# Regrouping the small products of a recurrence by shape and by array half

## The chip, the cores and the metric

The kernel runs on one core of one Trainium2 chip. The metric is the device time of the program in microseconds (us), the median of several runs. The profile comes from one further execution of the same program, taken by the hardware profiler.

## The reference

Two layers of a block on 256 tokens of width 2048, in fp32: a mixer with two branches (an RWKV-7 recurrence with 16 heads of 64, and a causal attention with 8 heads), a cross attention on 256 memory rows, and a feed-forward part of width 8192. The change lies in the recurrence, which the reference writes token by token:

```python
def step(state, inp):
    r_t, w_t, k_t, v_t, kk_t, b_t = inp
    sa = jnp.einsum('bhvk,bhk->bhv', state, -kk_t)
    state = (state * w_t[:, :, None, :]
             + sa[..., :, None] * b_t[:, :, None, :]
             + v_t[..., :, None] * k_t[:, :, None, :])
    return state, jnp.einsum('bhvk,bhk->bhv', state, r_t)
```

Each head then has a group norm over its 64 outputs, a bonus term and a gate. The result is joined with the attention's output and goes through the output projection.

## The kernel before

**Main line and fibers.** Instructions of TensorE are issued in the order in which the program emits them. The large products are the main line (`gemmA`, `gemmB`, `gemm_seq`): weights of 512 columns are loaded as fp32 (`raw`), split by ScalarE into a rounded high part `wh` (line 298) and by VectorE into the rest `wl` (lines 300 and 304), and multiplied in three terms, which accumulate in PSUM tiles named `g`. Everything else on TensorE runs in fibers: Python generators that yield an estimate in microseconds, or an event, until their next TensorE instruction can run. `K.clk` is a planned clock: `mm` (line 237) adds an estimated cost for each product, and after each k tile of a large product (128 rows of the weights) `poll` steps the fibers whose time has come. The planner thus weaves small products between large ones. Fibers put their products in PSUM tiles named `x`, from a pool of four banks (`xps`); `half` is half of such a bank. All products go through `mm`, so their line in the profile is L243; transpositions are L248. The other engines take their instructions in their own order.

**The recurrence in chunks.** A layer's 16 heads are worked in two groups of eight (`g`), the 256 tokens in four chunks (`c`) of 64. Of a group's eight heads four (`h` = 0) lie on partitions 0 to 63 of the operands and four (`h` = 1) on partitions 64 to 127; `i` counts the four, `j` = 4h + i. The fibers of one group, in order:

- `f_group` (line 606) makes the decayed operands `AR` and `BK`, then runs `f_inner` (line 690). For each chunk `f_inner` multiplies `BK` by `AR` head by head (64 rows by 128 columns), first the four heads of one row half (`q` = 0), masked by VectorE into `W` (line 706), then a yield (line 708), then the other four. ScalarE copies parts of `W` to `G` (line 710). After the four chunks come the bonus, the transposed operands `tok` and the inverse, whose forward substitution `f_fs` (line 776) is on VectorE.
- `f_v` (line 800) prepares the values; in layer 1 it mixes in the first layer's values (lines 826 to 830, GpSimd, then VectorE) and transposes them.
- `f_chain` (line 859) takes the state from chunk to chunk in three products of eight heads each: `X` (line 873, from `W` and `V`), `SA` (line 882, from `UT` and `X`) and, but for the last chunk, the new state `Sn` (line 892, from `tok` and `V`). List `HD` (line 857) is the order of the heads: the four of the first half, then the four of the second. The halves of `X` and of `Sn` go to different column halves of the array (partitions 0 to 63 and 64 to 127 of one PSUM tile), those of `SA` come from different row halves. After chunks 1 and 3 it spawns `f_out`.
- `f_out` (line 908) is called for 128 tokens (`t`), two chunks. For each head half and chunk it computes, head by head, `W` times `VS` (128 rows by 64 columns of the array) and, in all chunks but the first, `AR` times the state (64 by 64), added to the same output (lines 926 and 928). VectorE takes mean and difference from the output (lines 929 to 931), a yield follows for each half, then group norm, transposition of `oc`, gate (`gup`, `gl`) and split.

The output projection `w_out` (line 1261) waits for `f_out` and the attention heads, k tile by k tile.

Of the kernel before, what the change touches and what calls it, by code (L numbers as in the profile page):

```python
# [12 lines left out]
ALU = mybir.AluOpType  # L13
AX = mybir.AxisListType

D, S, L = 2048, 256, 2
# [102 lines left out]
def pull(gen, n):  # L119
    """the first n of gen, now"""  # L120
    return [next(gen) for _ in range(n)]


def ahead(gen, n):
    """gen, made n items before their use"""
    buf = []
    for x in gen:
        buf.append(x)
        if len(buf) > n:
            yield buf.pop(0)  # L130
    yield from buf


class K:
    """PE instructions are issued in the order in which they are emitted here. The large products are the
    main line; everything else on PE runs in fibers, generators that yield an estimate of the time (us) until
    their next PE instruction can run, or the event they wait for."""
# [112 lines left out]
    def rsqrt(self, dst, src, scale, eps):  # L250
        """dst = (src*scale + eps)^-0.5, small tiles"""
        g = self.nc.gpsimd
        t = self.sm("rs", list(src.shape))
        g.tensor_scalar(out=t, in0=src, scalar1=scale, scalar2=eps, op0=ALU.mult, op1=ALU.add)
        g.tensor_tensor(out=dst, in0=t, in1=self.mhalf[:, : src.shape[-1]], op=ALU.pow)

# [1 line left out]
    def units(self, src, k0, nk, ncols, extra=None, heap=None, first=False):  # L258
        """yield (wh, wl, k tiles) of src[(k p), cols]"""
        nc = self.nc  # L260
# [19 lines left out]
    def hunits(self, w, nk, h0, nh, dh, hw, off):  # L280
        """units of head-strided columns: w[(k p), (h hw)] -> cols h*hw+off : +dh for nh heads"""
        nc = self.nc
# [32 lines left out]
    def gemm_seq(self, parts, lhs, order, need=None):  # L315
        """out[tok, N] = x @ w, parts: (units, number of k tiles, N, evac(t, ps)); order: (token tile, part, units) or
        (None, call, None);
        lhs(k, tok) -> (xh, xl) [128, 128]; need(k, tok): event before"""
# [25 lines left out]
    def gemmA(self, parts, nk, lhs, N, evac, need=None):  # L344
        """out[tok, N] = x @ w, both token tiles at a time; parts: generators of units"""
# [14 lines left out]
    def gemmB(self, units, nk, rhs, evac, nft=4, need=None):  # L360
        """out[feat, tok]: evac(pair, ps[128, 2, 256])"""
# [20 lines left out]
    def sumsq(self, srcs, name="ss"):  # L382
        """srcs: list of [128, n] APs -> [128, 1] sum of squares"""
# [16 lines left out]
    def toT(self, src, gain, U, t, j, nk=4):  # L400
        """src [128 tok, nk*128] -> k tiles 4j.. of U at the tokens of t, split; gain [128, k tiles]"""
# [23 lines left out]
    def load_bc(self, vec):  # L425
        """[2048] -> four [128, 512] tiles, the same on every partition"""
# [7 lines left out]
    def tiles4(self, s="y"):  # L434
        """[tok tile][512 columns]"""
# [10 lines left out]
    def f_pre(self, tag, l, h, t, gain, U, rstd, y=None, part=None):  # L446
        """h[t] += rms_norm(y[t]), then U (raw h * gain, transposed) and rstd[t] of h"""
# [13 lines left out]
    def finish(self, y, part, h, t):  # L461
        """h[t] += rms_norm"""
# [9 lines left out]
    def shift2(self, ps, scale_bc, mus, dests):  # L472
        """token shift of ps [P, n, 256] feature-major; dests: n [R, 256] APs"""
# [17 lines left out]
    def f_small(self, l, z, rstd, sm):  # L491
        """after the decay, learning rate, gate and value-residual columns z"""
        nc = self.nc
        yield ("z", l)
        # rstd[tok], the same on every partition
# [62 lines left out]
    def shift_gemm(self, l, g, c0, mu, U, sm, dst, key):  # L558
        """dst[128, 4, 256] = token shifted columns c0 + 512 g .. of the in projection, feature major"""
# [13 lines left out]
    def f_lora(self, l, g, sm, R):  # L573
        """lw = log decay, token major; a, feature major"""
# [8 lines left out]
        # -exp(-.5) * sigmoid(w0 + tanh(wl) @ w_up)  # L583
# [7 lines left out]
        # sigmoid(a0 + al @ a_up)  # L591
# [14 lines left out]
    def f_group(self, l, g, sm, R):  # L606
        """eight heads (columns 512 g ..): decayed operands, bonus, inverse"""
# [9 lines left out]
        # 1 / |kk| per head and token  # L617
# [25 lines left out]
        for i in range(4):  # L643
# [12 lines left out]
            # cumulative decays  # L656
# [33 lines left out]
    def f_inner(self, l, g, R, prods):  # L690
        """per chunk the masked products W [(b, k; s), head, (a, r; t)], the token-major b~, k~,
        and (I - Aab)^-1, transposed, in UT [(heads 0-3, 4-7; s), chunk, head, t]"""
# [5 lines left out]
        for c in range(4):  # L698
            W = self.t4("W", [128, 8, 128])
            for q in range(2):  # L700
                ps = self.xps().rearrange("p (h t) -> p h t", h=4)
                rows = slice(64 * q, 64 * q + 64)
                for i in range(4):
                    self.mm(ps[:, i, :], BK[i // 2][rows, i % 2, c].rearrange("p a b -> p (a b)"),
                            AR[i // 2][rows, i % 2, c].rearrange("p a b -> p (a b)"), True, True)
                nc.vector.tensor_tensor(out=W[:, 4 * q : 4 * q + 4, :], in0=ps, in1=mw, op=ALU.mult)
                if q == 0:
                    yield (0.60, 1.1)[g]
# [14 lines left out]
        # bonus, over the heads' keys  # L723
# [41 lines left out]
        # a~ in the place of Aab, above Aak  # L765
# [10 lines left out]
    def f_fs(self, l, g, N, T, R):  # L776
        """the inverses of the unit lower triangular 32 x 32 blocks, by forward substitution:
        T[(parity of the column, half, unit), row, column // 2]"""
# [13 lines left out]
        # Ud[(half, s), unit, t] = T[t, s], Tr[(half, t), unit, s] = T[t, s]  # L792
# [7 lines left out]
    def f_v(self, l, g, sm, R):  # L800
        """values: residual, token-major copies VS, bonus * v + lnx_b"""
# [55 lines left out]
    HD = [(h, i, 4 * h + i, slice(64 * h, 64 * h + 64)) for h in range(2) for i in range(4)]  # L857

    def f_chain(self, l, g, sm, R, O):
        """the state from chunk to chunk"""  # L860
# [6 lines left out]
        for c in range(4):  # L867
            W, V, St = Ws[c], VS[c], Sts[c]
            # X = A~ S' + Aak V, S' over V's rows 0-63
# [7 lines left out]
            # SA = T X, over V's rows 0-63  # L877
            for h in range(2):
                psa = self.half()
                rows = slice(64 * h, 64 * h + 64)  # L880
                for i in range(4):
                    self.mm(psa[0:64, i, :], UT[rows, c, i, :], X[rows, i, :], True, True)
                if h:
                    nc.vector.tensor_copy(out=V[0:64, 4:8, :], in_=psa[0:64])
                else:
                    nc.scalar.copy(out=V[0:64, 0:4, :], in_=psa[0:64])
            yield (1.8, 1.8)[g]
            if c < 3:
                # S' <- gamma (S' + B~^T SA + K~^T V)
# [18 lines left out]
    def f_out(self, l, g, t, sm, R, Sts, oh, ol):  # L908
        """O = R~ S' + Arb SA + Ark V, token major, group norm over the head dim, bonus, gate"""
# [8 lines left out]
        oc = self.t2("oc", [128, 4, 2, 64])  # L918
        for h in range(2):
            po = self.half()  # L920
            rows = slice(64 * h, 64 * h + 64)
            for c in (2 * t, 2 * t + 1):
                orow = slice(64 * (c % 2), 64 * (c % 2) + 64)
                for i in range(4):
                    j = 4 * h + i
                    self.mm(po[orow, i, :], Ws[c][:, j, 64:128], VS[c][:, j, :], True, c == 0, True)
                    if c:
                        self.mm(po[orow, i, :], AR[i // 2][rows, i % 2, c, 1, :], Sts[c][rows, i, :], False, True, True)
# [3 lines left out]
            yield (0.5, 0.5)[g]  # L932
# [25 lines left out]
    def mix(self, l, U, rstd, units):  # L958
        """the mixed tokens, transposed and split: a function of the k tile and the token tile"""
# [47 lines left out]
    def rope(self, x, t, dst, n, e):  # L1007
        """x, dst [128, n, 64]"""
# [511 lines left out]
```

## Time and profile before

| | |
|---|---|
| time, median of 3 runs | 2681.59 us (2678.27 to 2687.71) |
| the profiled execution, span | 2672.5 us |
| the two stretches with the recurrence's products | 130 to 452 us (layer 0), 1452 to 1781 us (layer 1) |
| ScalarE, VectorE, GpSimd busy | 45%, 60%, 16% |
| moved by DMA | 456.69 MB, mean 171 GB/s |

The profiled execution has no time of its own beside its span; the median of the runs stands 9.1 us above it. In the views `PE` is TensorE's matmuls, `PEld` its weight loads, `DVE` VectorE, `ACT` ScalarE, `POOL` GpSimd, `SP` the queue that issues the weight loads from memory. A matmul's length is its latency; matmuls overlap, so how fast they follow each other is read from their start times. In the timeline, neighbours of the same kind are merged into one row with their count. In windows the columns are the stretch, its length, busy time with the number of instructions that touch the stretch, granted clock of TensorE (1.00 is full), busy share of the DMA engines and GB/s.

### The profile page before, as it was taken

Reading aid. Unit: us, or ns where it says so; the run is one execution under the profiler, and the core shown is the slowest. Engines: PE = TensorE matmul, PEld = TensorE weight load, DVE = VectorE, ACT = ScalarE, POOL = GpSimd, SP = SyncE. Lnnn points to the kernel's source line nnn. Section 1 sums busy time; section 2 is a strip of 40 time slices with the busy share of each in tenths; the row PEclk is TensorE's granted clock in tenths of the full one; section 3 lists DMA queues with packets and bytes.
Section 4 is the critical chain, followed back from the end, with each engine's and each line's share of the span. In section 5 each row is a group of like instructions: output and inputs, shape, how many; then the busy total and the mean of one; then the engine's idle time right before and its main releaser. Section 6 shows DMA issues by size and latency. Waiting matters only on the chain. (4 is left out here: it accounts for less than half of the span.)

```text
span 2672.5 us, 42409 instructions
## 1 busy us (share of the span) xinstructions
PE 2597.2 (97%) x17458; PEld 2335.1 (87%) x17458; DVE 1595.9 (60%) x2445; ACT 1206.2 (45%) x1724; POOL 432.9 (16%) x597
## 2 busy tenths in 40 slices
PE   8999989999999999999999999999999999999997
PEld 7988877888998899889888898889799998999896
DVE  4775875766445545555667758756754455555545
ACT  5443443545444444444453535534454444444443
POOL 2313413402000000000034235112010000000000
PEclk9999999999999999999999999999999999999999
DMA  5443343654555555555654443455455555555564
GB/s 197 150 153 114 97 156 127 227 190 143 189 186 190 189 183 185 191 189 193 212 166 150 141 126 97 159 181 180 151 167 184 185 190 190 188 188 189 189 205 142
DMA packets 250851, 456.69 MB, mean 171 GB/s; under 512 B 19269, under 2 KB 52421, under 8 KB 250657
## 3 DMA queue, kind: packets, MB, share of 16 engines
q1 hardware_dynamic: 241280, 422.77, 48.2%
q0 software_dynamic: 9376, 31.21, 3.6%
q8 instruction: 137, 2.24, 0.3%
q14 instruction: 58, 0.47, 0.1%
HBM read 444.50 MB, written 9.44 MB: 170 GB/s over the span
## 5 line engine op out<-in xcount | busy, mean ns | idle before, releaser
L298 ACT CAST wh<-raw 128x1024 fp32r<-128x1024 f32 (+2 forms) x804 | 831.9, 1042 | 1033.9 <-PE g L243 692.7
L300 DVE TENSOR_TENSOR wl<-raw,wh 128x1024 fp32r<-128x1024 f32 x480 | 586.6, 1224 | 568.4 <-ACT wh L298 565.7
L243 PE MATMUL g<-uh,wh 128*128 128x256 f32 x2816 | 809.3, 287 | 2.1 <-ACT wh L298 2.1
L243 PE MATMUL g<-uh,wl 128*128 128x256 f32 x2816 | 798.8, 284 | 1.7 <-DVE wl L304 1.7
L243 PE MATMUL g<-ul,wh 128*128 128x256 f32 x2816 | 798.3, 284 | 0.0
L304 DVE TENSOR_TENSOR wl<-raw,wh 128x512 fp32r<-128x512 f32 (+2 forms) x648 | 435.3, 712 | 194.5 <-ACT wh L298 194.0
L243 PEld LDWEIGHTS g<-uh,wh 128*128 128x128 f32 x2816 | 542.0, 192 | 7.8 <-ACT wh L298 2.9
L243 PEld LDWEIGHTS g<-uh,wl 128*128 128x128 f32 x2816 | 542.0, 192 | 5.2 <-DVE wl L304 2.7
L243 PEld LDWEIGHTS g<-ul,wh 128*128 128x128 f32 x2816 | 541.8, 192 | 0.0
L243 PE MATMUL g<-wh,hdh 128*128 128x512 f32 x1024 | 398.9, 390 | 1.6 <-ACT wh L298 1.6
L243 PE MATMUL g<-wl,hdh 128*128 128x512 f32 x1024 | 398.8, 389 | 1.5 <-DVE wl L300 1.5
L243 PE MATMUL g<-wh,hdl 128*128 128x512 f32 x1024 | 398.4, 389 | 0.0
L1366 POOL TENSOR_TENSOR rl<-rl 128x512 f32<-128x512 f32 x60 | 61.3, 1041 | 1174.4 <-ACT rl L1365 1174.4
L243 PEld LDWEIGHTS g<-wh,hdh 128*128 128x128 f32 x1024 | 192.3, 188 | 41.8 <-ACT wh L298 2.4
L243 PEld LDWEIGHTS g<-wl,hdh 128*128 128x128 f32 x1024 | 192.3, 188 | 41.3 <-DVE wl L300 2.1
L243 PEld LDWEIGHTS g<-wh,hdl 128*128 128x128 f32 x1024 | 192.2, 188 | 39.9
L243 PE MATMUL g<-wh,uh 128*128 128x256 f32 (+3 forms) x320 | 113.5, 355 | 11.9 <-ACT wh L298 6.9
L243 PE MATMUL g<-wl,uh 128*128 128x256 f32 (+3 forms) x320 | 109.5, 342 | 8.3 <-DVE wl L304 8.2
L243 PE MATMUL g<-wh,ul 128*128 128x256 f32 (+3 forms) x320 | 108.1, 338 | 2.3 <-POOL ul L413 1.5
L1369 DVE TENSOR_TENSOR hdl<-rl,hdh 128x512 fp32r<-128x512 f32 x60 | 47.7, 795 | 67.6 <-ACT hdh L1368 67.6
L1386 DVE SCALAR_TENSOR_TENSOR y<-g,s,y 128x512 f32<-128x512 f32 x112 | 78.9, 743 | 7.5 <-PE g L243 7.4
L243 PEld LDWEIGHTS g<-wh,uh 128*128 128x128 f32 x320 | 62.2, 194 | 18.8 <-ACT wh L298 8.1
(342 smaller groups left out, 3174.1 us busy)
## 6 DMA issues: line engine op xcount, KB each, us to landing
raw<-in_w_ff_dram SPq DMA_DIRECT2D x256, 1024.0 KB, 5.3
raw<-in_w_in_dram SPq DMA_DIRECT2D x56, 1024.0 KB, 5.3
raw<-in_w_out_dram SPq DMA_DIRECT2D x32, 1024.0 KB, 5.1
raw<-in_wk_mem_dram SPq DMA_DIRECT2D x8, 1024.0 KB, 5.3
raw<-in_wq_mem_dram SPq DMA_DIRECT2D x8, 1024.0 KB, 6.0
raw<-in_wv_mem_dram SPq DMA_DIRECT2D x8, 1024.0 KB, 5.3
raw<-in_wo_mem_dram SPq DMA_DIRECT2D x8, 1024.0 KB, 5.0
raw<-in_w_in_dram SPq DMA_DIRECT2D x7, 896.0 KB, 5.3
```

The costliest lines, as they stand in the source:

```text
L243: return self.nc.tensor.matmul(out, lhsT, rhs, start=start, stop=stop, skip_group_check=skip)
L298: nc.scalar.copy(out=wh, in_=raw)
L300: nc.vector.tensor_tensor(out=wl, in0=raw, in1=wh.bitcast(F32), op=ALU.subtract)
L304: nc.vector.tensor_tensor(out=wl[:, s], in0=raw[:, s], in1=wh[:, s].bitcast(F32), op=ALU.subtract)
L1366: nc.gpsimd.tensor_tensor(out=r, in0=r, in1=r, op=ALU.mult)
L1369: nc.vector.tensor_tensor(out=hl[:, 2 * q : 2 * q + 2, :], in0=r, in1=o.bitcast(F32), op=ALU.subtract)
L1386: nc.vector.scalar_tensor_tensor(out=o, in0=ps, scalar=s2[t], in1=o, op0=ALU.mult, op1=ALU.add)
```

## The change

It reorders TensorE's small products in `f_inner`, `f_chain` and `f_out`, and removes or joins yields between them; all other lines of the diff are comments. In `f_inner` both row halves of a chunk are computed head by head in turn into two PSUM tiles, and the two maskings and no yield follow. `HD` now has the two halves of the heads in turn. In `f_chain` the `SA` products of both halves are issued in turn into two tiles, then copied. In `f_out` all products of `W` and `VS` come first, the two chunks (column halves) in turn, then all products with the state, in the order of four different quarters of the array; both halves of the output stay in PSUM, only the first product on a tile's rows clears, the VectorE operations of both halves follow, and one yield of 1.0 stands for two of 0.5.

```diff
@@ f_inner
             W = self.t4("W", [128, 8, 128])
+            pw = [self.xps().rearrange("p (h t) -> p h t", h=4) for _ in range(2)]
+            for i in range(4):
+                for q in range(2):
+                    rows = slice(64 * q, 64 * q + 64)
+                    self.mm(pw[q][:, i, :], BK[i // 2][rows, i % 2, c].rearrange("p a b -> p (a b)"),
+                            AR[i // 2][rows, i % 2, c].rearrange("p a b -> p (a b)"), True, True)
             for q in range(2):
-                ps = self.xps().rearrange("p (h t) -> p h t", h=4)
-                rows = slice(64 * q, 64 * q + 64)
-                for i in range(4):
-                    self.mm(ps[:, i, :], BK[i // 2][rows, i % 2, c].rearrange("p a b -> p (a b)"),
-                            AR[i // 2][rows, i % 2, c].rearrange("p a b -> p (a b)"), True, True)
-                nc.vector.tensor_tensor(out=W[:, 4 * q : 4 * q + 4, :], in0=ps, in1=mw, op=ALU.mult)
-                if q == 0:
-                    yield (0.60, 1.1)[g]
+                nc.vector.tensor_tensor(out=W[:, 4 * q : 4 * q + 4, :], in0=pw[q], in1=mw, op=ALU.mult)
@@ HD and f_chain
-    HD = [(h, i, 4 * h + i, slice(64 * h, 64 * h + 64)) for h in range(2) for i in range(4)]
+    HD = [(h, i, 4 * h + i, slice(64 * h, 64 * h + 64)) for i in range(4) for h in range(2)]
...
-            for h in range(2):
-                psa = self.half()
-                rows = slice(64 * h, 64 * h + 64)
-                for i in range(4):
-                    self.mm(psa[0:64, i, :], UT[rows, c, i, :], X[rows, i, :], True, True)
-                if h:
-                    nc.vector.tensor_copy(out=V[0:64, 4:8, :], in_=psa[0:64])
-                else:
-                    nc.scalar.copy(out=V[0:64, 0:4, :], in_=psa[0:64])
+            psa = [self.half() for _ in range(2)]
+            for h, i, j, rows in self.HD:
+                self.mm(psa[h][0:64, i, :], UT[rows, c, i, :], X[rows, i, :], True, True)
+            nc.scalar.copy(out=V[0:64, 0:4, :], in_=psa[0][0:64])
+            nc.vector.tensor_copy(out=V[0:64, 4:8, :], in_=psa[1][0:64])
@@ f_out
+        pos = [self.half() for _ in range(2)]
+        orow = lambda c: slice(64 * (c % 2), 64 * (c % 2) + 64)
+        for h, i, j, rows in self.HD:
+            for c in (2 * t, 2 * t + 1):
+                self.mm(pos[h][orow(c), i, :], Ws[c][:, j, 64:128], VS[c][:, j, :], i == 0, c == 0, True)
+        for i in range(4):
+            for h, e in ((0, 0), (1, 1), (0, 1), (1, 0)):
+                c, rows = 2 * t + e, slice(64 * h, 64 * h + 64)
+                if c:
+                    self.mm(pos[h][orow(c), i, :], AR[i // 2][rows, i % 2, c, 1, :], Sts[c][rows, i, :], False, True, True)
         for h in range(2):
-            po = self.half()
-            rows = slice(64 * h, 64 * h + 64)
-            for c in (2 * t, 2 * t + 1):
-                orow = slice(64 * (c % 2), 64 * (c % 2) + 64)
-                for i in range(4):
-                    j = 4 * h + i
-                    self.mm(po[orow, i, :], Ws[c][:, j, 64:128], VS[c][:, j, :], True, c == 0, True)
-                    if c:
-                        self.mm(po[orow, i, :], AR[i // 2][rows, i % 2, c, 1, :], Sts[c][rows, i, :], False, True, True)
+            po = pos[h]
...
-            yield (0.5, 0.5)[g]
+        yield (1.0, 1.0)[g]
```

## The prediction

> **What bounds the kernel now.** I read the page first (span and busy shares), then who waited for whom on TensorE, the chain of waits near the regrouped products, the groups by line and form, and last the timeline of TensorE around single blocks.
>
> The page, the longest waits of TensorE (total us, times, longest), one piece of the chain (start, length), and the forms of the four products that the change regroups (x instructions | busy, mean ns of one):
>
> ```profile
> span 2672.5 us, 42409 instructions
> PE 2597.2 (97%) x17458; PEld 2335.1 (87%) x17458; DVE 1595.9 (60%) x2445; ACT 1206.2 (45%) x1724; POOL 432.9 (16%) x597
> ...
> PE g L243 <- DVE wl L304: 13.5, 21, 3.0
> ...
> 1753.59 25.28 PE x L243 x124
> ...
> L243 PE MATMUL x<-VS,W 128*64 128x64 f32 x448 | 45.3, 237 | 0.2 <-issue 0.2
> L243 PE MATMUL x<-AR,BK 64*128 64x128 f32 x256 | 38.8, 294 | 2.4 <-DVE W L706 2.4
> L243 PE MATMUL x<-Sn,AR 64*64 64x64 f32 x192 | 31.8, 247 | 0.0
> L243 PE MATMUL x<-X,UT 64*64 64x64 f32 x256 | 15.4, 224 | 0.0
> ```
>
> TensorE works 97% of the span, and its longest wait for anything sums to 13.5 us. The chain runs over small products (x) as it does over large ones (g). So a microsecond of TensorE time is a microsecond of span, unless something then comes late. One product of the code is two matmul instructions here. A mean of 237 ns is a latency: what counts is how far apart the starts lie, and that is read from the timeline (start, length, name, x merged instructions).
>
> **f_out (the output product).** Layer 1, second half of the heads, tokens 128 to 255, first head half; below the dots one half of tokens 0 to 127 in layer 0:
>
> ```profile
> 1755.70 0.39 PE L243 MATMUL x<-wl,oh 128*128 128x512 f32 x1
> 1755.92 0.39 PE L243 MATMUL x<-wh,ol 128*128 128x512 f32 x1
> 1756.24 0.33 PE L243 MATMUL x<-VS,W 128*64 128x64 f32 x2
> 1756.50 0.32 PE L243 MATMUL x<-Sn,AR 64*64 64x64 f32 x2
> 1756.76 0.33 PE L243 MATMUL x<-VS,W 128*64 128x64 f32 x2
> ...
> 1760.35 0.50 PE L243 MATMUL x<-wh,oh 128*128 128x512 f32 x1
> ...
> 233.76 0.68 PE L243 MATMUL x<-VS,W 128*64 128x64 f32 x10
> ...
> 236.16 1.25 PE L243 MATMUL x<-VS,W 128*64 128x64 f32 x26
> ```
>
> The two shapes alternate product by product, 0.26 us each: 16 take 1760.35 - 1756.24 = 4.11 us, both head halves 8.22. Tokens 0 to 127 alternate in one chunk of two (the first has no state): 2.40 us a half, 4.80 for both. What would the same products cost without alternating? The first step of the state chain shows it; the counts are instructions in flight in each short stretch:
>
> ```profile
> 211.44 0.96 PE L243 MATMUL x<-VS,W 64*64 64x64 f32 x16
> 212.33 0.39 PE L243 MATMUL g<-uh,wh 128*128 128x256 f32 x1
> ...
> 211.43:211.72 0.29, 0.28 (x5) 1.00 0.00 0
> 211.69:211.70 0.01, 0.01 (x4) 1.00 0.00 0
> 211.90:211.91 0.01, 0.01 (x7) 1.00 0.00 0
> 212.16:212.17 0.01, 0.01 (x4) 1.00 0.00 0
> ...
> 219.82:219.83 0.01, 0.01 (x7) 1.00 0.11 1
> ...
> 201.05 2.21 PE L243 MATMUL x<-Tr,W 32*32 32x32 f32 x64
> 203.19 0.38 PE L243 MATMUL g<-uh,wh 128*128 128x256 f32 x1
> ```
>
> Eight instructions on one column half stand ahead of eight on the other. Five start in the first 0.29 us, 58 ns apart. At both ends of the block four are in flight, in its middle seven: there both halves run at once, about 30 ns from start to start (58 / 2; by 224 ns over 7, 32). So a change of half costs no pause, two halves overlap, and one half by itself is the limit for the first and the last 0.29 us. The 32 x 32 products show that 64 instructions in a row can start (203.19 - 201.05) / 64 = 33 ns apart. A product of two instructions at 58 ns takes 0.116 us; alternating with another shape it took 0.26, so a change of shape costs 0.14 us.
>
> After the change tokens 128 to 255 take 64 instructions at 30 ns and three changes of shape (in, between, out): 1.92 + 0.42 = 2.34 us, and tokens 0 to 127 48 instructions, 1.86 us. Saved: 8.22 - 2.34 = 5.88 and 4.80 - 1.86 = 2.94, together 8.8 us a layer and half of the heads, four times: 35.3 us. One block instead of two also saves an entry and an exit, 0.2 us by the rows of the next part, eight times: 1.6.
>
> **f_chain.** 0.89 us a block of 16 instructions, 44 blocks (4 + 4 + 3, four times). Alternating halves double up in the first and last 0.29 us: 0.58 / 2 is 0.29, of which I take 0.28: 12.3 us saved.
>
> **f_inner.** The masked products, 64 rows by 128 columns, one row half per block, with large products between the blocks:
>
> ```profile
> 132.75 0.40 PE L243 MATMUL g<-wh,ul 128*128 128x512 f32 x1
> 133.08 1.16 PE L243 MATMUL x<-AR,BK 64*128 64x128 f32 x8
> 134.16 0.50 PE L243 MATMUL g<-wh,uh 128*128 128x512 f32 x1
> 134.50 0.39 PE L243 MATMUL g<-wl,uh 128*128 128x512 f32 x1
> ```
>
> Steady large products of this form start 0.22 us apart (1755.92 - 1755.70 above). A block costs 134.16 - 133.08 = 1.08, plus 0.11 going in (0.33 for 0.22) and 0.12 coming out (0.34 for 0.22): 1.31 us. After the change one block of 16 does the work of two, the row halves side by side in different PSUM banks. No trace row has row halves of this shape together; the products with X and UT, also on row halves, have the mean of 224 ns of the column-half ones, so I take full overlap: 16 blocks vanish, 21.0 us. The other end is one after the other, only the 0.23 us saved: 3.7 us.
>
> The sum on TensorE is 35.3 + 1.6 + 12.3 + 21.0 = 70.2 us.
>
> **The clock.** After the long alternating blocks TensorE's granted clock halves. The first and the last of four such stretches behind tokens 128 to 255 (length, busy, granted clock); the lengths are 3.42, 3.41, 3.41 and 6.83:
>
> ```profile
> 266.54:269.96 3.42, 3.42 (x18) 0.50 0.00 0
> ...
> 1764.99:1771.82 6.83, 6.83 (x22) 0.50 0.29 80
> ```
>
> 17.07 us at half pace lose 8.5. A block of 2.3 us in place of 8.2 gives less cause; as the trace also shows such stretches elsewhere, I count 5.
>
> **What is handed back.** f_inner's yield between the head halves goes, so a chunk meets one k tile of large products instead of two, and takes two of the four x banks at once; the next chunk has the other two. Queued behind a late bank on TensorE is everything, large products too. What can come late:
>
> ```profile
> 1461.43 1.75 DVE L830 TENSOR_TENSOR vT<-vT,vf 128x512 f32<-128x512 f32 x1 [2.52 <-POOL vf L829]
> ...
> 1466.12 0.66 PE L248 MATMUL x<-Id,vT 128*128 128x128 f32 x4 [1.35 <-DVE W L706]
> ...
> 1472.74 0.58 PE L243 MATMUL x<-AR,BK 64*128 64x128 f32 x1 [2.36 <-DVE W L706]
> ...
> 275.00:370.00 95.00, 86.47 (x578) 76.95 (x577) 82.06 (x207) 48.04 (x95) 33.34 (x48) 0.98 0.41 128
> 1620.00:1700.00 80.00, 74.55 (x459) 65.48 (x458) 71.62 (x186) 41.45 (x82) 33.90 (x41) 0.96 0.49 151
> ...
> 1759.30 1.04 ACT L298 CAST wh<-raw 128x1024 fp32r<-128x1024 f32 x1 [4.62 <-DMA raw<-in_w_out_dram]
> ```
>
> In layer 1 the value residual holds VectorE 2.52 us for GpSimd, the masking of W stands behind it, and TensorE already waits 1.35 and 2.36 us: arriving there up to 4 x 1.31 = 5.2 us earlier is mostly longer waiting. Of 10.5 us in the two halves of layer 1 I give back 7. VectorE (third figure) has 13 and 8 us free in the stretches around the second half's f_inner: I give back 3 of layer 0's 5.2. In the output projection a weight tile came 4.62 us late by DMA, hidden under the long blocks of f_out that go: 4. Together 14; the bounds are 0 and 27.5 (10.5, 5.2, and the 5.9 of f_out twice).
>
> The f_out evacuations of both halves now follow the products, one half's three VectorE operations (about 1 us) later for the group norm, and the single yield of 1.0 replaces two of 0.5:
>
> ```profile
> 1775.81 0.69 DVE L940 TENSOR_TENSOR oc<-oc,grs 128x512 f32<-128x512 f32 x1
> ...
> 1778.71 0.60 PE L248 MATMUL x<-Id,oc 128*128 128x128 f32 x4
> ```
>
> The normed tile is ready 2.2 us ahead of its transposition, and that covers it; without cover it costs 1 us eight times. The DMAs of gup are issued where they were and used no sooner in the emission order. Nothing else moves between queues.
>
> **Result.** 70.2 + 5 - 14 = 61 us. The execution's span is 2672.5; 9.1 us separate it from the median of the runs, 2681.6, and I take them as constant: 2681.6 - 61 = 2621. Its own range: 2601 (no give-back, all 8.5 of the clock, 1.6 for four quarters at once) to 2639 (27.5 handed back, no clock).
>
> **Rivals.**
> (A) One matmul at a time: the overlap of seven in flight lasts only as long as something queued ahead feeds it, and a long run starts every 58 ns. f_out then saves 1.60 + 4.09 four times, plus 1.6: 24.4; f_inner 3.7; f_chain nothing; with 5 for the clock and 6 handed back 27 us: 2655. Against it stand the 33 ns of the 32 x 32 products; for it, that those are smaller. 0.10. The Trainium skill, TensorE: Matmul & The Clock Gate, section Back-to-back issue gap, has a sequencer limit of about 62 ns a matmul with hardware decode off; the 33 ns row speaks against that limit here.
> (B) Only row halves overlap. Column-half neighbours share all rows of the array, and their weight loads may have to wait. Then the X and state products of f_chain (28 blocks by 0.28, 7.8 us) and the first 32 instructions of each f_out (32 by 29 ns eight times, 7.4 us) save no more than the shape changes: 2636. The seven in flight at 211.90 and at 219.82, both column halves, speak against it. 0.10. The Trainium skill has this as a rule, on the same page, Part 3, The mechanism: weight loads overlap running matmuls only when the row group differs; the two rows with seven in flight disagree, in short bursts.
> (C) Slower: a change of half inside long runs is paid like a change of shape, 0.26 us a product. f_chain's blocks take 8 x 0.26 = 2.08 instead of 0.89, +52 us; f_inner's 8 x (2 x 0.135 + 0.14) + 0.23 = 3.5 instead of 2 x 1.31, +14; f_out 6.2 instead of 5.0 and 8.3 instead of 8.4, +4: 2681.6 + 70 = 2752. At no pause the same order still saves 20 us (A's 24.4 + 3.7, less the 0.17 us that each of 44 blocks gains from its middle now); from 20 to -70 over 0.14 us the turn lies near 30 ns a change. The seven in flight right after a change speak against it; only the diagonal order of f_out's second part has no row. 0.04.
> (D) Nothing moves, because TensorE waits for VectorE as much as it saves: the free 13 and 8 us do not allow it outside these stretches. 0.02, 2682.
>
> **Chances.** The forecast has 0.74, A and B 0.10 each, C 0.04, D 0.02. Of faster by over 0.3% (8 us; about what a measurement of this kernel can tell from no change) that makes 0.94, within 0.02, slower 0.04. The range reaches from 2601 over A to 2656, and leaves out C, D and the tails.
>
> **What would show it.** Right: an f_out block of tokens 128 to 255 about 2.3 us long with one change of shape; 16 blocks of x<-AR,BK with 16 instructions in 1.1 us; f_chain's blocks at 0.61; no half clock behind f_out; TensorE's waits for W and wl up by some 10 us. Wrong: AR,BK blocks near 2 us (A), X and state blocks still 0.89 while the SA ones shrink (B), gaps of 0.15 us at each change of half (C), or waits for wl, W and vT up by over 30 us (D).

## The result and the profile after

The median of the changed kernel is 2622.23 us (2620.17 to 2623.62, 4 runs); the kernel before, run on the same chip, has 2684.65 us (2678.27 to 2691.56, 4 runs). The ratio is 0.9769, 95% interval 0.9749 to 0.9788: faster by 62.4 us. The forecast was 2621.

The page of the kernel after, its span and TensorE's share:

```profile
span 2619.1 us, 42411 instructions
PE 2528.3 (97%) x17458; PEld 2280.7 (87%) x17458; DVE 1593.2 (61%) x2445; ACT 1205.2 (46%) x1724; POOL 435.4 (17%) x597
```

TensorE works 97% of the span as before, with as many instructions, and the span is 53.4 us shorter (2672.5 before). So the time came out of TensorE's own blocks. The timeline of TensorE shows which. First f_out: tokens 128 to 255 of layer 1's second half of the heads (three lines), then tokens 0 to 127 of layer 0's first half; start, length, name, x merged instructions.

```profile
1709.62 1.15 PE L243 MATMUL x<-VS,W 128*64 128x64 f32 x32
1710.71 0.69 PE L243 MATMUL x<-Sn,AR 64*64 64x64 f32 x32
1711.33 0.50 PE L243 MATMUL x<-wh,oh 128*128 128x512 f32 x1
...
222.21 1.15 PE L243 MATMUL x<-VS,W 128*64 128x64 f32 x32
223.29 0.68 PE L243 MATMUL x<-Sn,AR 64*64 64x64 f32 x16
223.90 0.69 PE L243 MATMUL x<-VS,W 128*64 128x64 f32 x16
```

The 64 instructions of both head halves take 1711.33 - 1709.62 = 1.71 us, where they took 8.22; 2.34 was forecast. Tokens 0 to 127 take 223.90 - 222.21 = 1.69 (before 4.80, forecast 1.86). The product with W, 32 instructions, takes 1.09 us; the product with the state, 32 on four quarters, only 0.62, as long as 16 of them take in the fifth line. One change of shape lies between, as was said.

Then f_inner's block of 16 and f_chain's blocks, each with the large product that follows:

```profile
135.21 1.16 PE L243 MATMUL x<-AR,BK 64*128 64x128 f32 x16
136.30 0.50 PE L243 MATMUL g<-wh,uh 128*128 128x512 f32 x1
...
1696.72 0.69 PE L243 MATMUL x<-VS,tok 128*64 128x64 f32 x16
1697.34 0.50 PE L243 MATMUL g<-wh,mh 128*128 128x512 f32 x1
...
1704.70 0.68 PE L243 MATMUL x<-X,UT 64*64 64x64 f32 x16
1705.32 0.50 PE L243 MATMUL g<-wh,mh 128*128 128x512 f32 x1
```

Sixteen masked instructions take 1.09 us, as eight did (1.08): full overlap of the row halves. Nine of the 16 blocks have this length; the other seven take 1.68 to 4.80 us, as they run at half clock, hold a wait or follow one. SA (x<-X,UT) and the state product (x<-VS,tok) take 0.62 in place of 0.89. The state product uses all rows of the array, and its neighbours differ by the column half alone, so column halves overlap as row halves do, and rival (B) falls. The Trainium skill, TensorE: Matmul & The Clock Gate, Part 3, The mechanism, lets weight loads overlap running matmuls only where the row group differs; this row disagrees (0.62 against 0.89 us for the same 16 instructions).

What TensorE waited for (us in total, times, longest), after, longest sums first, and then the rows of before that answer to them:

```profile
PE g L243 <- DVE wl L304: 14.5, 20, 3.1
PE g L243 <- ACT wh L298: 10.8, 6, 6.1
PE x L248 <- DVE vT L488: 6.2, 4, 3.6
PE g L243 <- ACT qn L1099: 6.2, 2, 3.7
...
PE x L243 <- ACT qrT L1063: 5.4, 2, 3.2
PE x L243 <- DVE W L707: 4.6, 3, 2.3
...
PE x L248 <- DVE W L707: 2.2, 2, 1.9
```

```profile
PE x L248 <- DVE vT L488: 2.8, 4, 1.4
PE x L243 <- ACT qrT L1066: 2.7, 1, 2.7
PE g L243 <- ACT qn L1102: 2.6, 1, 2.6
PE x L243 <- DVE W L706: 2.6, 2, 2.4
PE x L248 <- DVE W L706: 1.8, 2, 1.3
```

W and vT went from 7.2 to 13.0 us, the weights hardly moved (13.5 to 14.5 for wl, 10.6 to 10.8 for wh), and the latent attention's operands qn and qrT doubled from 5.3 to 11.6. All rows of that view together go from 62.8 to 78.1.

The clock, by windows (length, TensorE's busy time, granted clock, DMA share, GB/s). First the 10 us behind the four blocks of tokens 128 to 255, then four of the stretches in which the clock halves now:

```profile
246.20:256.20 10.00, 9.85 (x90) 1.00 0.38 126
404.20:414.20 10.00, 10.00 (x53) 1.00 0.28 97
1549.30:1559.30 10.00, 9.85 (x90) 1.00 0.55 172
1711.30:1721.30 10.00, 10.00 (x53) 1.00 0.85 313
```

```profile
126.69:133.52 6.83, 6.39 (x29) 0.50 0.27 85
283.71:290.54 6.83, 6.24 (x38) 0.50 0.44 146
474.94:481.77 6.83, 5.99 (x29) 0.51 0.34 100
1433.97:1444.21 10.24, 7.62 (x30) 0.50 0.35 124
```

No half clock is left behind f_out. But in this pair of executions the stretches ahead of the kernel's end sum to 47.8 us before and after: they stand now at the values and the masked products (126.69, 283.71, 1433.97) and at the cross attention's start (474.94).

### The profile page after: what moved, and what is told of

It is laid out like the page before. It is cut to its first block, busy times and chain, and to the rows that moved or that the text cites. A ratio compares the mean times of both kernels' runs of the same rounds, so it can differ in the third digit from the quotient of the medians.

```text
span 2619.1 us, 42411 instructions
## 1 busy us (share of the span) xinstructions
PE 2528.3 (97%) x17458; PEld 2280.7 (87%) x17458; DVE 1593.2 (61%) x2445; ACT 1205.2 (46%) x1724; POOL 435.4 (17%) x597
## 4 chain that ended last, share of the span: by engine, by line
PE 65%; issue 12%; DVE 10%; DMA 7%; ACT 3%; POOL 3%; SPq 0%; ACTq 0%; DVEq 0%; POOLq 0%
PE g L243 57%; PE x L243 7%; DVE wl L304 3%; DMA raw<-in_w_ff_dram 2%; ACT wh L298 2%; DMA raw<-in_w_in_dram 1%; PE x L248 1%; DMA raw<-in_w_out_dram 1%; DVE h L469 1%; DVE wl L300 1%; DVE uf L411 1%; DMA raw<-in_wk_mem_dram 1%; DMA raw<-in_wq_mem_dram 1%; DVE T L784 0%; DVE fs L782 0%
## 5 line engine op out<-in xcount | busy, mean ns | idle before, releaser
L243 PEld LDWEIGHTS g<-wh,hdl 128*128 128x128 f32 x1024 | 192.7, 188 | 40.1
L1383 DVE SCALAR_TENSOR_TENSOR y<-g,s,y 128x512 f32<-128x512 f32 x112 | 78.9, 743 | 9.0 <-PE g L243 9.0
L243 PEld LDWEIGHTS g<-wh,uh 128*128 128x128 f32 x320 | 62.4, 195 | 19.9 <-ACT wh L298 8.3
```

The source lines that it names most:

```text
L243: return self.nc.tensor.matmul(out, lhsT, rhs, start=start, stop=stop, skip_group_check=skip)
L1383: nc.vector.scalar_tensor_tensor(out=o, in0=ps, scalar=s2[t], in1=o, op0=ALU.mult, op1=ALU.add)
```

## The experiments

Twelve kernels, each measured against the kernel before on its chip (medians there 2684.3 to 2686.5 us). To tell two things apart, the last columns split the mean span of the timed runs: span times mean granted clock is about what it would take at full clock, the rest is the most that the half clock can have cost (a stretch spent waiting costs nothing). The clock is recorded to three digits, 1.3 us of a span; on the three chips the kernel before has 2639.6 to 2640.5 in the first of these columns. Differences between kernels are of medians; where the chips differ, that by the ratios stands in brackets, and each ratio carries some 5 us.

| kernel | edit | median us | ratio, 95% interval | at full clock | clock |
|---|---|---|---|---|---|
| before (52 runs) | | 2684 to 2687 | 1 | 2640.1 | 43.9 |
| after | whole change | 2622.2 | 0.9769 (0.9749 to 0.9788) | 2590.1 | 30.1 |
| e1_inner | f_inner alone | 2679.6 | 0.9981 (0.9966 to 0.9996) | 2633.4 | 45.1 |
| e2_chain | f_chain alone | 2676.8 | 0.9972 (0.9957 to 0.9988) | 2630.4 | 45.0 |
| e3_out | f_out alone | 2653.3 | 0.9886 (0.9867 to 0.9906) | 2615.0 | 37.1 |
| e4_out_shape | f_out by shape, halves not in turn | 2665.2 | 0.9927 (0.9909 to 0.9944) | 2623.4 | 39.5 |
| l1_no_inner | whole without f_inner | 2645.1 | 0.9845 (0.9822 to 0.9867) | 2606.2 | 37.0 |
| l2_no_chain | whole without f_chain | 2635.6 | 0.9809 (0.9787 to 0.9830) | 2604.0 | 28.4 |
| l3_no_out | whole without f_out | 2665.4 | 0.9924 (0.9901 to 0.9948) | 2622.0 | 42.6 |
| v1_wide | whole, f_inner's chunks wider apart | 2634.1 | 0.9801 (0.9780 to 0.9823) | 2594.7 | 36.8 |
| x1_l1_mla | l1, latent attention's columns later | 2647.9 | 0.9861 (0.9839 to 0.9884) | 2608.8 | 37.7 |
| x2_v1_mla | v1, the same | 2650.8 | 0.9875 (0.9850 to 0.9899) | 2607.1 | 41.7 |
| v2_vlate | whole, values transposed later | 2628.1 | 0.9784 (0.9763 to 0.9806) | 2588.6 | 37.4 |
| v3_inner_seq | whole, f_inner's row halves not in turn | 2631.2 | 0.9798 (0.9774 to 0.9822) | 2593.6 | 34.6 |

The theory is that of the prediction: TensorE's issue is the bound, an instruction of 64 columns costs 58 ns to start, neighbours on other halves overlap, a change of shape costs 0.14 us, and part of what TensorE saves is handed back in waits. The rivals were that something other than the blocks makes the time, or that the parts act otherwise than their TensorE time says.

**e1_inner**: the f_inner part alone in the kernel before.

```
-            for q in range(2):
-                ps = ...
-                for i in range(4):
-                    self.mm(ps[:, i, :], ...)
-                nc.vector.tensor_tensor(out=W[...], in0=ps, in1=mw, op=ALU.mult)
-                if q == 0:
-                    yield (0.60, 1.1)[g]
+            pw = [...]
+            for i in range(4):
+                for q in range(2):
+                    self.mm(pw[q][:, i, :], ...)
+            for q in range(2):
+                nc.vector.tensor_tensor(out=W[...], in0=pw[q], in1=mw, op=ALU.mult)
```

> The kernel before with the f_inner part of the change alone: both row halves of a chunk in one block, no yield between. Theory (the gain is TensorE's time, less what VectorE, ScalarE and the clock hand back at the masked products): 16 blocks of 1.31 us go, 21 us of TensorE time, but TensorE then waits for vT, W and the attention's copies, and its clock halves behind those waits, as in the trace after (6.8 us at half clock at 126 and at 283 us, 10.2 us at 1434 us): net 5 to 13 us under the kernel before. Rival (the handing back has its place elsewhere, f_inner keeps its gain): 18 to 21 us under it. Second rival (the row halves overlap only in the trace's modelled ends): 4 us or less.

Measured: 2679.6, 4.7 us faster, just under the theory's 5 to 13. Nine of the 16 blocks have their 16 instructions in 1.09 us, the others wait or run at half clock as in the whole change, so TensorE saves its 21 before waits. TensorE's waits (sums over the span), then the place of the longest, layer 1's second half: TensorE's timeline, and VectorE's.

```profile
PE x L243 <- DVE W L707: 9.8, 5, 4.4
...
PE x L248 <- DVE W L707: 5.6, 4, 3.5
```

```profile
1648.77 2.67 PE L243 MATMUL x<-AR,BK 64*128 64x128 f32 x16 [4.37 <-DVE W L707]
1652.87 1.11 PE L248 MATMUL x<-Id,vT 128*128 128x128 f32 x4 [1.44 <-DVE W L707]
```

```profile
1642.87 1.77 DVE L829 TENSOR_TENSOR vT<-vT,vf 128x512 f32<-128x512 f32 x1 [1.31 <-POOL vf L828]
1645.79 1.19 DVE L829 TENSOR_TENSOR vT<-vT,vf 128x512 f32<-128x512 f32 x1 [1.15 <-POOL vf L828]
...
1648.03 1.28 DVE L707 TENSOR_TENSOR W<-x,C 128x512 f32<-128x512 f32 x2
...
1652.14 0.68 DVE L707 TENSOR_TENSOR W<-x,C 128x512 f32<-128x512 f32 x1
```

Before, W cost 4.4 us of waiting, here 15.4: the masking of W stands in VectorE's queue behind the value residual vT, which waits for GpSimd, and all of TensorE's queue behind the two banks that the masking would free. That is the hand-back of the prediction, 11 us of the 21, and near its places: this one has 7.4 of the 15.4 (0.2 before), layer 0's second half 4.1 (none before), and layer 1's first half has 3.9 (4.2 before). Another 5.2 us goes to a wait for ml that had been 0.4, and all waits together go from 62.8 to 78.9. In the whole change W's waits sum to 6.8, but at layer 0's second half TensorE now waits 3.6 us for vT where it waited for W here. W and vT together are 18.2 here and 18.5 in l3_no_out, both with the old f_out; 13.0 in the whole change and 14.9 in l2_no_chain, with the new one; and 15.4 in v2_vlate below, also with the new one.

**e2_chain**: the order of the heads in turn, and SA over both halves.

```
-    HD = [... for h in range(2) for i in range(4)]
+    HD = [... for i in range(4) for h in range(2)]
...
-            for h in range(2):
-                psa = self.half()
-                for i in range(4):
-                    self.mm(psa[0:64, i, :], ...)
+            psa = [self.half() for _ in range(2)]
+            for h, i, j, rows in self.HD:
+                self.mm(psa[h][0:64, i, :], ...)
```

> The kernel before with the order of heads HD and the SA products in turn, in f_chain alone. 44 blocks at 0.61 in place of 0.89 us are 12.3 us of TensorE time. Theory: f_chain lies where TensorE is never waiting, so nearly all of it shows, 10 to 13 us under the kernel before. Rival (each step of the chain is bound by the copies between its products, so that shorter products only wait longer): 0 to 4 us.

Measured: 7.5 us faster, between the theory and its rival. The blocks take 0.61 to 0.62 us as in the whole change, 12.3 us less of TensorE; at full clock the time falls by 9.7.

**e3_out**: the f_out part alone.

```
-            po = self.half()
-            for c in (2 * t, 2 * t + 1):
-                for i in range(4):
-                    self.mm(po[...], Ws..., VS...)
-                    if c:
-                        self.mm(po[...], AR..., Sts...)
+        for h, i, j, rows in [... for i in range(4) for h in range(2)]:
+            for c in (2 * t, 2 * t + 1):
+                self.mm(pos[h][orow(c), i, :], Ws..., VS...)
+        for i in range(4):
+            for h, e in ((0, 0), (1, 1), (0, 1), (1, 0)):
+                if c:
+                    self.mm(pos[h][orow(c), i, :], AR..., Sts...)
```

> The kernel before with the f_out part alone, its heads in turn. By the traces the output products take 38.7 us less on TensorE and one entry and exit less each (1.6). Theory: all of it shows, and the half clock behind tokens 128 to 255 goes too: 40 to 48 us under the kernel before, no half clock within 5 us behind f_out. Rival (the weights of the output projection come late when the long blocks go, and the clock halves for other reasons): 28 to 35 us.

Measured: 31.0 us faster, 25.1 of it at full clock. The blocks are those of the whole change (64 instructions in 1.71 us, 40 us less of TensorE). TensorE's waits for sq go from 1.6 to 6.0 us, for qn from 2.6 to 5.1, and all waits together from 62.8 to 73.7: 11 us are handed back. The 31 lie in the rival's range and under the theory's 40 to 48, but not for the rival's first reason: the waits for wl and wh, the weights, rise by 1.1 us only. Regrouping f_out is the largest part of the change by itself.

**e4_out_shape**: as e3, but chunk by chunk and head half by head half: grouped by shape, neighbours on the same half or quarter.

```
+        for c in (2 * t, 2 * t + 1):
+            for h in range(2):
+                for i in range(4):
+                    self.mm(pos[h][orow(c), i, :], Ws..., VS...)
+        for e in range(2):
+            for h in range(2):
+                for i in range(4):
+                    self.mm(pos[h][orow(c), i, :], AR..., Sts...)
```

> As e3_out, but only grouped by shape: the products of W and VS chunk by chunk (all eight heads on one column half, then all eight on the other), then those with the state, one quarter of the array after the other, four heads each. It tells the grouping by shape from the turn of halves. Theory, from 58 ns a start on one half and some overlap where the half changes: a block of tokens 128 to 255 takes about 3.2 us (1.7 in e3_out), one of 0 to 127 2.6, 30 us of TensorE time less than before, and the half clock goes as in e3_out: 8 to 12 us slower than e3_out. Rival (the turn of halves is all, a change of shape is cheap by itself): less than half of e3_out's gain.

Measured: 19 us faster, 12 less than e3. The same block in layer 1's second half; the large product follows 3.30 us after its start:

```profile
1757.65 1.90 PE L243 MATMUL x<-VS,W 128*64 128x64 f32 x32
1759.47 1.54 PE L243 MATMUL x<-Sn,AR 64*64 64x64 f32 x32
```

8.22 us became 3.30 by the grouping and 1.71 by the turn of halves. The single starts lie 58 ns apart here, save at a change of half or quarter, where three pairs start within 4 to 6. In turn, they come in pairs (6 and 52 ns), in the product with the state in fours (7, 7, 6 and 38 ns), a pair or a four every 58 to 59 ns. So the grouping has 19 of f_out's 31 us and the turn 12. The grouping counts here with what comes with it: one block for both head halves and one yield for two.

**l1_no_inner, l2_no_chain, l3_no_out**: the whole change with one part put back as it was; the edits are those above, reversed.

> The whole change without its f_inner part. The three parts alone gained 5.0, 7.5 and 30.6 us, 43 together, and the whole change 62: 19 us come from their being together. Theory (a stall or a half clock that one part causes falls on blocks that another part has shortened, and the two unchanged parts keep the clock halving in either kernel): with f_inner missing less than the sum is lost, 10 to 25 us slower than the whole change, 2632 to 2647 us, and the granted clock of its runs between that of before (0.984) and after (0.989). Rival (the parts add, and the measurement of the parts was off): 5 us slower than the whole change, 2627.

> The whole change without its f_chain part. Theory: f_chain's 12.3 us of TensorE time show in full, since without the other stalls nothing hands them back: 2632 to 2637 us, clock as in the whole change (0.988). Rival (additive): 7.5 us slower, 2630. Second rival (the chain's shorter blocks only lengthen waits): 2623 to 2626.

> The whole change without its f_out part. Theory: the long alternating blocks keep halving the clock, as in e1_inner and e2_chain (33 to 37 us lost at half clock budgeted in their traces' half-clock stretches behind f_out and elsewhere): 40 us of TensorE time and about 8 us of clock are missing, 2664 to 2674 us, granted clock 0.982 to 0.985, and half-clock stretches directly behind the four blocks of tokens 128 to 255. Rival (additive): 30.6 us slower, 2653, clock 0.987 or more.

Measured: without f_inner 22.8 us slower than the whole change (20), without f_chain 13.3 (11), without f_out 43.1 (42), all three inside their theory's range. But in l3_no_out only two of the four blocks of tokens 128 to 255 have a half clock at them, and not all four as expected. Alone the three parts had 4.7, 7.5 and 31.0, together 43; taken away from the whole they have 79 (73); the whole has 62. So the parts help each other.

By the table 8 of the 19 us between 43 and 62 come at full clock (6.7, 9.7 and 25.1 alone, 49.9 together) and 9 by the clock (-1.2, -1.1 and 6.8 alone, 13.8 together).

f_inner gains most from the others: about what its TensorE time says where f_out is short, a quarter of it where f_out is long. In the profiled executions it adds 16.1 us to all of TensorE's waits when alone (62.8 to 78.9) and takes 1.8 away beside the others (79.9 in l1_no_inner, 78.1): a difference of 17.9, as large as the 18 us between 4.7 and 22.8. W and vT are 6.1 of it (7.2 to 18.2 alone, 8.1 to 13.0 beside the others). The table gives only 9.3 of these 18 at full clock and 8.1 by the clock, so how they divide between waits and clock stays open.

Another piece of the waits is seen in l1_no_inner, where sq of ScalarE stands behind a rope of GpSimd (the rows are those of TensorE at the squares, and of the clock behind it):

```profile
257.54 3.57 PE L243 MATMUL x<-C,sq 128*128 128x2 f32 x16 [6.60 <-ACT sq L621]
```

```profile
253.00:266.60 13.60, 9.06 (x44) 8.84 (x46) 2.95 (x7) 4.16 (x8) 7.70 (x14) 0.50 0.29 98
```

That wait of 6.6 us and the 13.6 us of half clock around it are not in the whole change.

**v1_wide**: the whole change with f_inner's chunks two k tiles apart, which a theory of crowded maskings wanted.

```
-            yield (0.1, 0.1)[g]
+            yield (1.7, 1.7)[g]
```

> The whole change, but after each chunk of f_inner a yield of 1.7 in place of 0.1, so that two k tiles of large products stand between chunks again, as in the kernel before. Theory (what f_inner hands back comes from chunks that follow each other faster than VectorE masks them): TensorE's waits for W fall below 3 us (6.8 in the trace after), 2612 to 2619 us. Rival (the waits at f_inner are those for the values of layer 1 and come whatever the distance): 2620 to 2625 us.

Measured: 12 us slower than the whole change (9). W's waits do not fall (11.3 against 6.8 us), and the wait of 6.6 us for sq is back. The theory that more room between the chunks helps falls, and the rival's 2620 to 2625 is missed too.

**x1_l1_mla and x2_v1_mla**: in both kernels with that wait, the code that puts the ropes on GpSimd is emitted later, behind the squares.

```
     def f_mla_cols(self, l, cq, ckv, M):
-        yield 2.0
+        yield 12.0
```

> The change without its f_inner part, and f_mla_cols' first yield 2.0 raised to 12.0, so that in layer 0 the ropes on GpSimd (L1012 to L1015) are emitted after f_group's squares sq (L621) and not before. Without the delay TensorE waits 6.6 us for sq, sq waits 6.1 us for krt of GpSimd, and 13.65 us of half clock follow (6.8 lost). Theory (the worth of f_inner's part beside the others, 22.8 us where it has 5 alone, is in good part this one order of GpSimd before ScalarE, which the tight f_inner happens to avoid): sq waits for krt no more, TensorE's wait for sq goes from 6.6 to under 1, the half clock behind it goes, and the time falls by 8 to 13 us from 2645, to 2632 to 2637. Rival (the wait only moves to the next late thing, and the 22.8 are f_inner's own TensorE time): the wait may go, the time stays within 3 us of 2645.

> v1_wide (the whole change, f_inner's last yield 1.7 in place of 0.1) with f_mla_cols' first yield 12.0 in place of 2.0. v1_wide was 12 us slower than the whole change and shows the same 6.6 us wait for sq and 10.2 us of half clock behind it, which the whole change does not have. Theory: these two are its 12 us, so the time falls from 2634 to 2620 to 2625, that of the whole change. Rival (the wider spacing costs elsewhere, by waits for late products of f_inner): 2631 to 2636 with no wait for sq.

Measured: 2647.9 (2645.1 without the delay) and 2650.8 (2634.1 without it). The wait for sq is gone in both, and nothing was won. In both, TensorE now waits for cq, which the same delay made late (6.3 us in all). In x1_l1_mla the half clock is there again in two other places, and the second begins within that wait:

```profile
1583.49 1.09 PE L248 MATMUL x<-Id,cq 128*128 128x128 f32 x4 [5.42 <-DVE cq L1027]
```

```profile
277.80:284.60 6.80, 5.34 (x25) 0.50 0.00 0
1581.70:1588.50 6.80, 5.01 (x24) 0.50 0.00 0
```

So the theory that this one wait is what f_inner is worth beside the others falls, as does its use for v1_wide. In x1_l1_mla the rival held: the wait moved to the next late thing. x2_v1_mla is slower than both its ranges.

**v2_vlate**: the whole change, values transposed later, to take away its waits for vT.

```
-        if l:
-            yield (6.2, 6.2)[g]
+        yield 9.0 if l else 3.5
```

> The whole change, with the transposition of the values (f_v) later: in layer 0 a yield of 3.5 ahead of it where there was none, in layer 1 9.0 in place of 6.2. The whole change waits 6.2 us on TensorE for vT (3.6 of it in layer 0's second half). Theory (TensorE's waits at f_inner are the hand-back, and a later emission hides them): the waits for vT go from 6.2 to under 2.5 and the time falls by 3 to 8 us, to 2614 to 2619. Rival (the state chain starts later for it and the wait turns up there, or the next late thing takes its place): 2620 to 2626.

Measured: 6 us slower (4); the intervals of the two overlap. The waits for vT are gone, those for W are 14.2 us on the products alone:

```profile
PE x L243 <- DVE W L707: 14.2, 6, 6.3
```

At full clock it is 1.6 us faster than the whole change, about what the clock's three digits can tell, and it loses 7.3 to the clock. The rival's mechanism held, 2 us above its range; no kernel here beats the whole change.

**v3_inner_seq**: the whole change, one row half after the other within a block of 16.

```
-            for i in range(4):
-                for q in range(2):
+            for q in range(2):
+                for i in range(4):
```

> The whole change, but in f_inner's block of 16 the eight instructions of one row half come first and the eight of the other after them; yields, banks and maskings stay. It takes only the side-by-side of the row halves away, and a block of 16 should take two times a block of 8 without the gap between (1.085 us each, with an entry and an exit), about 2.0 us in place of 1.09. Theory (a TensorE microsecond there is one of span, less what lies under the waits for W and vT behind some blocks): 16 x 0.9 = 14.6 us more, less 2 to 5 under waits, 2631 to 2637. Rival (the blocks' length is hidden under the waits for VectorE at f_inner, and the worth of f_inner's part beside the others came from its order alone): 2620 to 2627 with the blocks at 2.0 all the same. Rival (the two halves overlap in this order as well, by what is in flight at once): blocks near 1.2 us and 2620 to 2626.

Measured: 8.9 us slower (8), on the theory's low edge. The block and the product behind it:

```profile
133.90 1.71 PE L243 MATMUL x<-AR,BK 64*128 64x128 f32 x16
135.54 0.50 PE L243 MATMUL g<-wh,uh 128*128 128x512 f32 x1
```

A block takes 1.64 us, 0.55 more than with the halves in turn; 16 of them are 8.8 us. The expected length of 2.0 was wrong, and the second rival has some of the truth: the starts lie 112 ns apart on one half, but where the half changes three pairs start within 4 to 6 ns, which makes 0.34 us. So of f_inner's 21 the turn of the halves has 8.8; the other 12 are one entry and exit for two and those three pairs. That the time rose by those 8.8 is no clean proof of one for one: the split of the runs gives 3.5 at full clock and 4.5 by the clock, and TensorE's waits fall from 78.1 to 72.2 us, W's from 6.8 to 2.9. So part of the longer blocks lies under waits, as the theory had it.

## Why the prediction was right, step by step

**What bounds the kernel** was right. TensorE's blocks got shorter by 73.4 us (40.1 + 12.3 + 21.0, below), and the span of the profiled pair by 53.4; no other engine's time changed by more than 3.

**f_out (35.3 + 1.6)** was too small: 8.22 - 1.71 = 6.51 and 4.80 - 1.69 = 3.11, both four times, are 38.5, with the entries 40.1. The term that was mis-sized is "64 instructions at 30 ns": 30 holds for the product with W, whose neighbours lie on two halves; the product with the state lies on four quarters and starts four in 58 ns. Of the 3.2 us between 35.3 and 38.5, 2.0 are that (the range had 1.6 for it). Most of the rest is the change of shape going in, 0.14 eight times: the sum counts it, but it lies ahead of the first start from which both 8.22 and 1.71 are read. The price of a change of shape, 0.14 us, held, and the starts of the alternating block before show its two parts: the first instruction of the new shape starts 151 ns behind the last of the old one, 93 more than 58, and the second 107 behind the first, 49 more.

**f_chain (12.3)** was right to the row: 0.61 forecast, 0.61 to 0.62 measured, on both kinds of half. The row that it came from was read too generously: in the block with seven in flight only three pairs overlap, at the change of half. That neighbours overlap all along when the halves take turns was an inference, and the runs bore it out.

**f_inner (21.0)** was right as TensorE time: 1.09 us for every block that neither waits nor runs at half clock, nine of the 16. "The other end ... 3.7 us" was too low even for halves that do not take turns, which save about 12 (21.0 - 8.8).

**The clock (+5)** was right in its place and wrong in its size and in what it left out. The half clock behind f_out is gone, all four stretches. In the profiled pair other stretches took their place, behind waits at f_inner, and the sum is unchanged. Over the timed runs, though, the share that goes with the clock falls from 43.9 to 30.1 us, up to 13.8, beyond the 8.5 that the prediction allowed. Which stretches the other executions have cannot be seen: each has one mean clock and no trace.

**"9.1 us separate it from the median of the runs ... and I take them as constant"** failed. In every run here the time outside the span is 1.7 to 1.8 us. The rest of the 9.1 was the luck of the profiled execution: its clock was 0.989, while the 52 runs of that kernel have spans from 2673.6 (0.989) to 2694.6 us (0.978), the longer the lower the clock, around a mean of 0.984. The kernel after ran at 0.988 to 0.989 in all four. Nine of the 62.4 us stem from that (53.4 in the spans of the profiled pair); the clock's term should have been taken from the runs' mean clock, not from the trace of one execution.

**What is handed back (14)** was too small: 73.4 - 53.4 = 20 in the profiled pair, 73.4 - 49.9 = 23.5 by the full-clock column, inside the bounds of 0 to 27.5. Of the places named, W and vT took 5.8 us more and the weights 1.2, where 10 and 4 were forecast; the latent attention's operands, which were not foreseen, took 6.3 in qn and qrT alone, while 3.1 for vv went. Its mechanism at the masked products shows in full only in e1_inner, where W's waits rise by 7.1 in layer 1's second half and by 4.1 in layer 0's, near the 7 and 3 that were forecast.

So the total hit because two terms that were too small, f_out's by 3 and the clock's by up to 9, met a hand-back that was too small by 6 to 10. That 2621 is within 1.3 us of the median is partly chance; the range was earned.

**The rivals.** One at a time (A) falls by the pairs and fours that start within 7 ns and by e4_out_shape, (B) by the state product's 0.62 us, (C) by the absence of any gap at a change of half, (D) by the span. What stays open: why the waits for W and vT are 18 us with the tight f_inner and the old f_out, and 13 to 15 with the new. The runs show that the waits move with the place at which each part arrives; they do not show a rule by which it could have been foretold, and the three attempts to place a wait better (v1_wide, x1_l1_mla, v2_vlate) each bought another one.

## What to carry to other kernels

On a TensorE-bound kernel, count changes of shape between neighbouring small products and neighbours that share a half: here a change cost 0.14 us, an instruction that takes turns with no other half 58 ns at 64 columns and 112 at 128, and those on the other half or on the three other quarters start inside that time. Price such a change by block lengths, and reckon with waits at places that move: here a quarter to a third of it came back; test parts by leaving them out of the whole as well as by doing them alone, since alone f_inner had 5 us and within the whole over 20. Take the clock and the time outside the span from several runs, not from the profiled one.

## What the runs showed of the hardware

Four 64 x 64 quarters run at once: 32 instructions in 0.62 us with entry and exit, 19 ns each, four starting within 20 ns every 58 to 59. The Trainium skill, TensorE: Matmul & The Clock Gate, section Back-to-back issue gap, has an issue floor of about 25 ns a matmul; that row disagrees for neighbours on different quarters, which start 6 to 7 ns apart.

The clock halves in stretches of 3.41 us or two, three or four times that, and not only where TensorE stands: the stretch that the prediction shows at 266.54 has it busy for all of its 3.42 us, behind a block in which two shapes alternated. In the four kernels with such blocks a half clock begins inside, or within 1.7 us behind, 13 of the 16 of tokens 128 to 255 (all four before and in e2_chain, three in e1_inner, two in l3_no_out). With the regrouped f_out, in ten kernels, none begins inside such a block or within 9 us behind it, 40 blocks in all.
